# The LRU's eight input chunks in two sets of four beside the incoming shift and scale units

## The chip, the cores and the metric

One NeuronCore of one Trainium2 chip. The metric is the time of one execution on the device in microseconds; the median of three runs of the kernel before is 2256.2 us (2254.24 to 2256.78).

## The reference, cut to what matters

Two layers of a decoder trunk on 256 tokens of width 2048 in float32. Each layer has a token mixer and a squared-ReLU MLP, each with a layer norm behind it, and each is modulated by a shift, a scale and a gate that come from a condition vector. Layer 0's mixer is the recurrent block (RG-LRU), layer 1's a sparse attention. What the change touches is the first modulation and the recurrent block:

```python
mod = jnp.einsum('bd,jde->bje', cond, ada_w[layer]) + ada_b[layer]
shift, scale, gate = jnp.split(mod, 3, axis=-1)
h = x * (1.0 + scale[:, 0, None]) + shift[:, 0, None]
y_br, x_br = jnp.split(h @ w_in, 2, axis=-1)
xc = conv_b + sum(xp[:, k:k + seq] * conv_w[k] for k in range(CONV_WIDTH))
gates = jnp.einsum('bsnd,jnde->jbsne', xb, gate_w)
...
u = jnp.sqrt(-jnp.expm1(2.0 * log_a)) * (i * xc)
_, hs = lax.associative_scan(_linear_combine, (a, u), axis=1)
y = (jax.nn.gelu(y_br) * hs) @ w_out
x = _layer_norm(DN_ALPHA * x + (1.0 + gate[:, 0, None]) * y, ln_w[layer, 0], ln_b[layer, 0])
```

`xp` is x_br with three rows of zeros in front and `xb` is xc in eight blocks of 256 columns, each with its own gate matrices. The gates go through a sigmoid and become a and i.

## The kernel before

Every product is computed in float32 by three matmuls (`mm3`, L193): each operand is cut into a high part (rounded on ACT, L137 for weights, L529 for activations) and a low part (the difference, on VectorE, L138 and L530). A weight unit is 1 MB: four k tiles of 128 rows by 512 columns; a piece is one k tile of it. A unit lands in one of six raw slots (`RAW`), is cut in two halves of 1024 columns, and lies in a ring of 16 pieces (`RING`), four units, until TensorE has used it.

All DMAs are issued on SP's queue in the order of one list, `stream`. Its items are weight units ("w"), units of the modulation's weights ("a": one VectorE instruction, L120, multiplies a 1 MB unit with the condition and sums it, which gives 128 columns of a shift, scale or gate), units that TensorE multiplies directly ("p", L379, for the first gate), the recurrent gates' matrices ("n", L873), and loads that take no slot ("d": here x, L364). `Builder` walks a clock of its own (`step`, 1.31 us for a piece, 3 us for the arrival of a unit) to decide where in the program an item is consumed (`pump`) and when tasks go on (`spawn`, `until`). The compiler then orders each engine's queue by its own estimate; each engine works through its queue in that order.

For the LRU's input, the activation is h, transposed: 16 k tiles in groups (`GROUPS0`). For each group the stream has its shift units, its part of x, its scale units, and then the weight parts of four output chunks, two of x_br (4 and 5) and two of y_br (0 and 1). When a group's last scale unit is done, `modulate` (L478) makes scale and shift (L461 to L470), modulates x on ACT (L488) and splits it. `gemm_ws_outer` (L212) runs the four chunks group by group, all eight PSUM banks holding their sums. Then `conv_done` (L816) and `gelu_done` (L840) read the banks, and `gates` (L859) computes the recurrent gates of chunks 0 and 1: 16 matmuls into four banks, then Tanh, Exp and Sqrt on ACT and products and a scan on VectorE, ending in Q, the operand of lru_out. The other two chunk pairs follow, 16 k tiles each (L921 to L924), each with its gate block. Beside them stand the 16 units of the first gate and the 8 shift and scale units of the MLP's first group (`merge`, L345). lru_out (`proj`, L635) runs four column blocks of 512, with both row halves in turn per k tile, but in the last block one half after the other ("end"); 8 more shift and scale units stand beside it. The layer norm and the MLP follow.

Work tiles of 4 KB per partition come from one pool of 20 (`NS4`, L71); PSUM banks from two tags of four, "g" and "m".

## Time and profile before

| | |
|---|---|
| median of three runs | 2256.2 us |
| profiled execution, its own time | 2254.88 us |
| its span | 2253.1 us |
| TensorE busy | 2156.2 us, 96% |
| weight loads of TensorE busy | 1926.7 us, 86% |
| VectorE busy | 1638.1 us, 73% |
| ACT busy | 1059.4 us, 47% |
| moved by DMA | 625.02 MB, mean 277 GB/s |
| chain that ended last | TensorE 86%, VectorE 8%, ACT 2%, DMA 1% |

PE is TensorE, PEld its weight loads, DVE VectorE, SP the engine that issues the DMAs. Times are us from the first instruction. A busy share is an average over the whole span; what a wait costs is read where it stands. The duration that a row gives one instruction can reach a little into the next one's, so the distance from start to start is the shorter price. Tiles have the program's names without numbers: s is a work tile, g and m are PSUM banks, raw, whi and wlo a unit and its two parts.

### The profile page before, as it was taken

The numbers are of one execution on the slowest core, as the hardware profiler recorded it, in microseconds if no ns is written. First come the engines' busy times: TensorE is split into PE (matmuls) and PEld (weight loads), VectorE is DVE, ScalarE is ACT, GpSimd is POOL, SyncE is SP. The second block draws the span as 40 slices with busy tenths as digits, with TensorE's granted clock in tenths as the row PEclk, the third lists the DMA queues.
The fourth block names the chain that finished last, engine by engine and source line by source line (L and its number), as shares of the span: only waits on it lengthen the run. The fifth ranks groups of instructions, "written<-read, shape, count | busy, mean of one in ns | idle before, by whom it ended". The sixth has DMA issues, their size and how long they took to land.

```text
span 2253.1 us, 34112 instructions
## 1 busy us (share of the span) xinstructions
PE 2156.2 (96%) x14093; PEld 1926.7 (86%) x14093; DVE 1638.1 (73%) x1959; ACT 1059.4 (47%) x1387; POOL 0.2 (0%) x4
## 2 busy tenths in 40 slices
PE   3799999899999999999999999999999999999997
PEld 3788877898998898898779988788989988988986
DVE  8898788797777677778887688667777544554566
ACT  2356563554554454354453345536544544543541
POOL 0000000000000000000000000000000000000000
PEclk9899999999999999999999999999999999999999
DMA  9988878689888887889788866355888655555671
GB/s 396 414 325 340 346 298 334 262 351 383 332 308 300 304 330 288 298 303 338 256 300 348 332 249 248 122 206 184 285 330 303 215 197 187 192 198 190 213 255 38
DMA packets 98775, 625.02 MB, mean 277 GB/s; under 512 B 10963, under 2 KB 13443, under 8 KB 27452
## 3 DMA queue, kind: packets, MB, share of 16 engines
q1 hardware_dynamic: 98620, 622.85, 74.0%
q8 instruction: 110, 1.80, 0.3%
q14 instruction: 45, 0.37, 0.0%
HBM read 614.36 MB, written 8.45 MB: 276 GB/s over the span
## 4 chain that ended last, share of the span: by engine, by line
PE 86%; DVE 8%; ACT 2%; issue 2%; DMA 1%; SPq 0%; DVEq 0%; ACTq 0%
PE g L196 27%; PE g L197 27%; PE g L195 26%; DVE raw L120 4%; DVE wlo L138 2%; PE m L1167 1%; PE m L1133 1%; ACT whi L137 1%; DMA raw<-in_ada 1%; PE m L197 0%; PE m L195 0%; ACT s L488 0%; PE m L196 0%; PE g L873 0%; PE m L1159 0%
## 5 line engine op out<-in xcount | busy, mean ns | idle before, releaser
L138 DVE TENSOR_TENSOR wlo<-raw,whi 128x1024 fp32r<-128x1024 f32 x721 | 870.5, 1222 | 448.3 <-ACT whi L137 447.3
L137 ACT ACTIVATE whi<-raw 128x1024 fp32r<-128x1024 f32 x721 | 755.0, 1057 | 860.5 <-PE g L197 439.2
L195 PE MATMUL g<-s,whi 128*128 128x256 f32 (+1 forms) x2768 | 773.6, 280 | 58.6 <-ACT s L529 57.5
L196 PE MATMUL g<-s,whi 128*128 128x256 f32 (+1 forms) x2768 | 771.5, 279 | 3.2 <-DVE s L530 3.2
L197 PE MATMUL g<-s,wlo 128*128 128x256 f32 (+1 forms) x2768 | 770.1, 279 | 1.9 <-DVE wlo L138 1.8
L195 PEld LDWEIGHTS g<-s,whi 128*128 128x128 f32 (+1 forms) x2768 | 522.4, 189 | 73.0 <-ACT s L529 58.6
L195 PE MATMUL g<-whi,s 128*128 128x512 f32 x1376 | 541.4, 394 | 7.6 <-ACT s L529 4.2
L196 PE MATMUL g<-wlo,s 128*128 128x512 f32 x1376 | 543.1, 395 | 2.1 <-DVE wlo L138 2.1
L197 PE MATMUL g<-whi,s 128*128 128x512 f32 x1376 | 543.9, 396 | 0.3 <-DVE s L530 0.3
L196 PEld LDWEIGHTS g<-s,whi 128*128 128x128 f32 (+1 forms) x2768 | 522.8, 189 | 7.2 <-DVE s L530 4.7
L197 PEld LDWEIGHTS g<-s,wlo 128*128 128x128 f32 (+1 forms) x2768 | 522.6, 189 | 5.4 <-DVE wlo L138 4.2
L120 DVE SCALAR_TENSOR_TENSOR raw<-raw,one,cond 128x2048 f32<-128x2048 f32 x176 | 411.5, 2347 | 44.9 <-DMA raw<-in_ada 44.6
L195 PEld LDWEIGHTS g<-whi,s 128*128 128x128 f32 x1376 | 259.6, 189 | 67.8 <-ACT s L529 5.9
L196 PEld LDWEIGHTS g<-wlo,s 128*128 128x128 f32 x1376 | 259.9, 189 | 62.7 <-DVE wlo L138 2.5
L197 PEld LDWEIGHTS g<-whi,s 128*128 128x128 f32 x1376 | 260.0, 189 | 56.4 <-DVE s L530 1.8
L195 PE MATMUL m<-s,whi 128*128 128x256 f32 x256 | 70.5, 277 | 0.2 <-ACT whi L137 0.2
L197 PE MATMUL m<-s,wlo 128*128 128x256 f32 x256 | 70.6, 276 | 0.0
L196 PE MATMUL m<-s,whi 128*128 128x256 f32 x256 | 70.6, 276 | 0.0
L488 ACT ACTIVATE s<-s,hB,hA 128x256 f32<-128x256 f32 x32 | 16.7, 592 | 101.2 <-DVE hA L464 75.8
L530 DVE TENSOR_TENSOR s<-t,s 128x512 fp32r<-128x512 f32 x78 | 53.3, 686 | 4.0 <-ACT s L529 3.8
L708 ACT ACTIVATE t<-g 128x512 f32<-128x512 f32 x58 | 33.9, 587 | 33.0 <-PE g L197 33.0
L195 PEld LDWEIGHTS m<-s,whi 128*128 128x128 f32 x256 | 48.0, 188 | 0.4 <-ACT whi L137 0.4
(196 smaller groups left out, 1046.9 us busy)
## 6 DMA issues: line engine op xcount, KB each, us to landing
raw<-in_mlp_w SPq DMA_DIRECT2D x256, 1024.0 KB, 5.0
raw<-in_ada SPq DMA_DIRECT2D x176, 1024.0 KB, 6.8
raw<-in_lru_in SPq DMA_DIRECT2D x28, 1024.0 KB, 6.3
raw<-in_nsa_kv SPq DMA_DIRECT2D x24, 1024.0 KB, 5.0
raw<-in_gate SPq DMA_DIRECT2D x16, 1024.0 KB, 10.9
raw<-in_lru_out SPq DMA_DIRECT2D x16, 1024.0 KB, 6.6
raw<-in_nsa_q SPq DMA_DIRECT2D x16, 1024.0 KB, 6.2
raw<-in_nsa_out SPq DMA_DIRECT2D x16, 1024.0 KB, 5.2
```

Of the source, the lines that this page charges most:

```text
L120: nc.vector.scalar_tensor_tensor(r, r, self.one, self.cond, op0=OP.mult, op1=OP.mult, accum_out=it.col)
L137: nc.scalar.activation(hi, src, AF.Copy)
L138: nc.vector.tensor_tensor(out=lo, in0=src, in1=hi.bitcast(F32), op=OP.subtract)
L195: mm(out, lhi, rhi, start=start, stop=False, skip_group_check=True)
L196: mm(out, lhi, rlo, start=False, stop=False, skip_group_check=True)
L197: mm(out, llo, rhi, start=False, stop=stop, skip_group_check=True)
L488: SC.activation(x[:, j, :], x[:, j, :], AF.Identity, scale=hA[s][:, k:k + 1], bias=hB[s][:, k:k + 1])
L530: V.tensor_tensor(out=lo, in0=src, in1=hi.bitcast(F32), op=OP.subtract)
L708: SC.activation(r2, banks[b], AF.Relu)
L1133: T.matmul(ps, qT[:, h, 128 * t:128 * t + 128], kT[g // 2][:, g % 2, :, 0:K], start=True, stop=True)
L1167: T.matmul(po, vt[br][:, kt, 128 * g:128 * g + 128], pT[:, br, kt], start=first, stop=False)
```

## The change

The eight chunks make two sets (`SETS0`): chunks 4, 0, 5, 1 and chunks 6, 2, 7, 3. The first group of four k tiles becomes two of two, the last two of two become one of four. `PLAN0` gives the order on TensorE: set 0 over k tiles 0 to 3, set 1 over 0 to 3 and 4 to 7, set 0 over 4 to 15, set 1 over 8 to 15. A set that stops before its last k tile copies its banks into work tiles (ACT); when it ends, the rest is added to them (VectorE), and convolution and GELU then read the work tile, not PSUM. The stream has set 1's parts merged with the shift and scale units of the next groups. All four gate blocks follow the whole input, each with three of the first gate's units behind it and the last four at the end; a block waits in the builder's clock until the block two before it is finished (`fin`), and its square root goes into xc's tile. The MLP's first 8 shift and scale units move from beside the input to lru_out, which then has 16.

```diff
--- before.py
+++ after.py
@@ -33,7 +33,9 @@
 NS4 = 20
 NS2 = 6
 LNACT = (0, 2)
-GROUPS0 = ((0, 4), (4, 8), (8, 12), (12, 14), (14, 16))
+GROUPS0 = ((0, 2), (2, 4), (4, 8), (8, 12), (12, 16))
+SETS0 = ((4, 0, 5, 1), (6, 2, 7, 3))
+PLAN0 = ((0, GROUPS0[:2], False), (1, ((0, 4), (4, 8)), False), (0, GROUPS0[2:], True), (1, ((8, 12), (12, 16)), True))
 GROUPS1 = ((0, 4), (4, 8), (8, 12), (12, 16))
 UNIT_US = 3.0
 
@@ -225,6 +227,27 @@
                 if k1 == NK:
                     done(b)
 
+    def gemm_ws_sets(self, act, plan, kinds, part):
+
+        for q, groups, final in plan:
+            k_first, k_last = groups[0][0], groups[-1][1] - 1
+            bs = [None] * len(kinds)
+            for k0, k1 in groups:
+                for c, kind in enumerate(kinds):
+                    if k0 == k_first:
+                        bs[c] = [self.bank([128, 2, 256], kind) for _ in range(2)]
+                    b = bs[c]
+                    for k in range(k0, k1):
+                        ahi, alo = act(k)
+                        whi, wlo = self.piece(self.cons)
+                        for f in range(4):
+                            sl = slice(128 * f, 128 * f + 128)
+                            self.mm3(b[f // 2][:, f % 2, :], whi[:, sl], wlo[:, sl], ahi, alo, k == k_first and f % 2 == 0, k == k_last and f % 2 == 1)
+                        self.take()
+                        self.step(1.31)
+                    if k1 == k_last + 1:
+                        part(q, c, b, final)
+
     def gemm_as(self, act, done, stagger=None, kind="g"):
         b = [self.bank([128, 512], kind) for _ in range(2)]
         if not stagger:
@@ -400,24 +423,30 @@
     def w_part(name, ix, k0, k1):
         return Item("w", a[name][ix + (k0 // 4,)][:, 512 * (k0 % 4):512 * (k0 % 4) + 512 * (k1 - k0)], width=512 * (k1 - k0))
 
-    for k0, k1 in GROUPS0:
+    def w_set(q, k0, k1):
+        return [w_part("lru_in", (i,), k0, k1) for i in SETS0[q]]
+
+    def in_group(k0, k1):
         ks = range(k0, k1)
-        stream += ada_items(0, 0, ks)
-        if k0 % 4 == 0:
-            stream.append(x_item(k0 // 4))
-        stream += ada_items(0, 1, ks, hook(("h0", k0, k1)))
-        stream += [w_part("lru_in", (i,), k0, k1) for i in (4, 0, 5, 1)]
-    lru_in = [N("lru_gate", 0), N("lru_gate", 1)]
-    for c in (2, 3):
-        lru_in += [W("lru_in", 4 + c, g) for g in range(4)] + [W("lru_in", c, g) for g in range(4)] + [N("lru_gate", c)]
+        x = [] if k0 % 4 else [x_item(k0 // 4)]
+        return ada_items(0, 0, ks) + x + ada_items(0, 1, ks, hook(("h0", k0, k1)))
+
+    for k0, k1 in GROUPS0[:2]:
+        stream += in_group(k0, k1) + w_set(0, k0, k1)
+    stream += merge(w_set(1, 0, 4), in_group(4, 8))
+    stream += merge(w_set(1, 4, 8) + w_set(0, 4, 8), in_group(8, 12))
+    stream += merge(w_set(0, 8, 12), in_group(12, 16))
+    stream += w_set(0, 12, 16) + w_set(1, 8, 12) + w_set(1, 12, 16)
+    gate0 = gate0_items()
+    for c in range(4):
+        stream += [N("lru_gate", c)] + gate0[3 * c:3 * c + 3]
+    stream += gate0[12:]
     lru_out = [W("lru_out", n, g) for n in range(4) for g in range(4)]
     def ss_group(k0, k1):
         ks = range(k0, k1)
         return ada_items(1, 0, ks) + ada_items(1, 1, ks, hook(("h1", k0, k1)))
 
-    gate0, ss0 = gate0_items(), ss_group(*GROUPS1[0])
-    stream += merge(lru_in, [it for i in range(8) for it in (gate0[2 * i], ss0[i], gate0[2 * i + 1])])
-    stream += merge(lru_out, ss_group(*GROUPS1[1]))
+    stream += merge(lru_out, ss_group(*GROUPS1[0]) + ss_group(*GROUPS1[1]))
     for i, (k0, k1) in enumerate(GROUPS1):
         if i > 1:
             stream += ss_group(k0, k1)
@@ -858,7 +887,7 @@
 
     def gates(c):
         d = L[c]
-        B.until(lambda: "xs" in d)
+        B.until(lambda: "xs" in d and (c < 2 or "fin" in L[c - 2]))
         xc = d["xs"]
         banks = {}
         for b in range(2):
@@ -892,7 +921,7 @@
             SC.activation(e, e, AF.Copy, scale=0.5, bias=0.5)
             n = B.t4([128, 4, 256])
             V.scalar_tensor_tensor(n, tr, 1.0, e, op0=OP.add, op1=OP.mult)
-            sq = B.t4([128, 4, 256])
+            sq = xc
             SC.activation(sq, tr, AF.Sqrt)
             yield 1.3
             V.scalar_tensor_tensor(n, n, 2.0, e, op0=OP.subtract, op1=OP.mult)
@@ -913,14 +942,28 @@
             split(hi, lo, g2)
             for f in range(4):
                 Q[4 * c + f] = [hi[:, f, :], lo[:, f, :], 3]
+            d["fin"] = True
         B.spawn(task())
 
-    B.gemm_ws_outer(act, [conv_done(0), gelu_done(0), conv_done(1), gelu_done(1)], "ggmm", GROUPS0)
-    gates(0)
-    gates(1)
-    for c in (2, 3):
-        B.gemm_ws(act, conv_done(c))
-        B.gemm_ws(act, gelu_done(c))
+    sums = {}
+
+    def part(q, c, banks, final):
+
+        if not final:
+            sums[q, c] = B.t4([128, 4, 256])
+        t = sums[q, c]
+        halves = [t[:, 2 * b:2 * b + 2, :] for b in range(2)]
+        for o, p in zip(halves, banks):
+            if final:
+                V.tensor_tensor(out=o, in0=o, in1=p, op=OP.add)
+            else:
+                SC.activation(o, p, AF.Copy)
+        if final:
+            i = SETS0[q][c]
+            (conv_done(i - 4) if i >= 4 else gelu_done(i))(halves)
+
+    B.gemm_ws_sets(act, PLAN0, "ggmm", part)
+    for c in range(4):
         gates(c)
 
     z = [None] * 4
```

## Rows read from the trace of the kernel before

**Rows 1.** Windows: length, busy us (count) of PE, PEld, DVE, ACT, POOL; clock, DMA share, GB/s.
```profile
0.00:37.85 37.85, 0.00 (x1) 0.01 (x1) 29.20 (x71) 8.02 (x13) 0.20 (x4) 1.00 0.96 385
37.85:152.71 114.86, 97.29 (x768) 95.42 (x769) 105.20 (x120) 45.28 (x59) 0.00 (x0) 0.93 0.99 398
152.71:295.25 142.54, 136.21 (x1027) 114.87 (x1025) 111.64 (x136) 89.31 (x133) 0.00 (x0) 1.00 0.81 315
295.25:390.12 94.87, 92.79 (x384) 74.40 (x384) 84.97 (x92) 43.16 (x42) 0.00 (x0) 0.96 0.87 333
441.00:473.00 32.00, 32.00 (x283) 31.82 (x281) 25.42 (x30) 11.68 (x17) 0.00 (x0) 1.00 0.88 348
310.00:390.00 80.00, 80.00 (x344) 64.57 (x342) 70.19 (x77) 30.34 (x29) 0.00 (x0) 1.00 0.90 346
```

**Rows 2.** Waits of TensorE, 0 to 400 us: total, times, longest.
```profile
PE g L195 <- ACT s L529: 53.2, 4, 37.8
```

**Rows 3.** Chain that ended last, 20 to 48 us: start, us, what.
```profile
21.59 2.27 DVE raw L120 x2
...
24.31 9.09 DVE raw L120 x8
```

**Rows 4.** Timeline, 62 to 72.2 us: start, us, instruction, count, idle before and releaser.
```profile
65.68 0.08 DVE L120 DVE_READ_ACCUMULATOR raw<-raw,one,cond 128x1 f32 x1
...
66.20 2.07 ACT L488 ACTIVATE s<-s,hB,hA 128x256 f32<-128x256 f32 x4 [21.78 <-DVE hA L464]
68.18 1.04 ACT L137 ACTIVATE whi<-raw 128x1024 fp32r<-128x1024 f32 x1
...
69.25 1.23 DVE L138 TENSOR_TENSOR wlo<-raw,whi 128x1024 fp32r<-128x1024 f32 x1 [3.09 <-ACT whi L137]
...
70.22 0.79 PE L195 MATMUL g<-s,whi 128*128 128x256 f32 x2 [6.65 <-ACT s L529]
...
71.67 0.58 PE L196 MATMUL g<-s,whi 128*128 128x256 f32 x1 [0.66 <-DVE s L530]
```

**Rows 5.** Windows, clock after that wait; columns as in the first group.
```profile
68.40:75.20 6.80, 4.33 (x18) 4.03 (x19) 5.95 (x6) 6.80 (x8) 0.00 (x0) 0.50 1.00 400
```

**Rows 6.** Timeline of VectorE, 318 to 376 us.
```profile
318.85 4.63 DVE L138 TENSOR_TENSOR wlo<-raw,whi 128x1024 fp32r<-128x1024 f32 x4
...
367.06 1.39 DVE L665 TENSOR_TENSOR s<-g,s 128x512 f32<-128x512 f32 x2 [2.82 <-PE g L197]
368.37 1.28 DVE L670 SCALAR_TENSOR_TENSOR s<-t,s 128x512 f32<-128x512 f32 x2
...
370.76 4.62 DVE L138 TENSOR_TENSOR wlo<-raw,whi 128x1024 fp32r<-128x1024 f32 x4
```

**Rows 7.** Instructions of VectorE by line, 145 to 318 us: busy, mean ns | idle before.
```profile
L834 DVE SCALAR_TENSOR_TENSOR s<-g,cols,s 128x255 f32<-128x255 f32 (+2 forms) x36 | 14.3, 473 | 2.6 <-ACT s L832 2.6
L906 DVE TENSOR_TENSOR_SCAN s<-s,s 128x256 f32<-128x256 f32 x16 | 9.8, 672 | 0.0
L901 DVE TENSOR_TENSOR s<-s,s 128x1024 f32<-128x1024 f32 x4 | 4.9, 1224 | 0.3
```

**Rows 8.** Instructions of ACT by line, 145 to 318 us.
```profile
L886 ACT ACTIVATE s<-s,spm 128x256 f32<-128x256 f32 x16 | 9.0, 609 | 0.0
...
L883 ACT ACTIVATE s<-g,gb 128x256 f32<-128x256 f32 x16 | 6.8, 469 | 2.6 <-PE g L873 2.5
...
L846 ACT ACTIVATE s<-g 128x512 f32<-128x512 f32 x6 | 3.6, 596 | 30.5 <-PE g L197 30.3
```

**Rows 9.** Timeline of TensorE, fourth gate block and the gate unit behind it.
```profile
283.86 1.89 PE L873 MATMUL g<-s,raw 128*128 128x256 f32 x8
...
290.86 1.04 PE L379 MATMUL m<-raw,condT 128*1 128x512 f32 x8
```

**Rows 10.** Timeline of ACT in the same block: the table load and what follows.
```profile
299.00 1.28 ACT L896 ACT_TABLE_LOAD   x1
300.29 1.06 ACT L896 ACTIVATE s<-s 128x1024 f32<-128x1024 f32 x1
```

## The prediction

> **What bounds the kernel now.** I read the shares of busy time first, then the windows by stage, the waits of TensorE, and the chain and the timeline where TensorE stands still. TensorE is busy 96% of the span, so all there is to win is its idle time and the stretches at the lower clock. The windows [rows 1] say where these are. Before 37.85 us TensorE does nothing. In the first stage (to 152.71, the first four input chunks beside the 32 shift and scale units) it is busy 97.3 of 114.9 us, VectorE 105.2, and the DMA engines are at 0.99. In the second (gates, chunks 2 and 3, to 295.25) it is busy 136.2 of 142.5, in the third (lru_out, to 390.12) 92.8 of 94.9: there TensorE is the bound.
>
> TensorE's waits in the first stage end with the rounded activation: 53.2 us in four waits, 37.8 of it at the start [rows 2]. The chain shows what stands before that: eight shift and scale products per four k tiles on VectorE, 2.27 us each (9.09 for four) [rows 3]. The timeline has the end of a group: ACT modulates for 2.07 us, rounds a weight, rounds the activation; VectorE waits 3.09 us meanwhile, and TensorE comes 6.65 us after its last matmul [rows 4], with a granted clock of 0.50, the lower level of 1.2 GHz, for the next 6.8 us [rows 5]: 3.4 us lost. A group on VectorE is 8 x 2.27, four weight units at 2.3 (four halves take 4.63 [rows 6]), and 4.6 for the wait, the sums and the activation's low part: 32.0 us. From 37.8 to 70.2 the trace has 32.4, so this sum is some 0.4 short per group. The first stage is a queue on VectorE, with the DMA close behind.
>
> **The change, part by part.** Times count from the start of the profiled span (2253.1 us; that execution's own time is 2254.9, the median of the runs 2256.2, so 1.3 is added at the end).
>
> (1) First groups of two k tiles. Four shift and scale units instead of eight stand before the first matmul; the fourth ends at 23.9 [rows 3], and with half the modulation TensorE starts near 27, not 37.85. Worth 0 by itself: it only comes earlier to the next wait for the same queue.
>
> (2) VectorE up to the last of the 32 units. Behind the fourth stand 28 units (63.6 us), 20 weight units (45.8; 8 more than before stand ahead of this point), and the ends of two short groups (3.1 each) and two long ones (4.6): 23.9 + 63.6 + 45.8 + 15.4 + 4 x 0.4 = 150.5. The DMAs to there, in order on SP's one queue, are 54 units of 1.05 MB and 1.5 MB of constants; 385 GB/s to 37.85 and 398 after it [rows 1] bring them by 147: hidden, by 3 us. TensorE's part is five groups of 192 matmuls at 0.113 (283 in 32 us [rows 1]), 21.7 us each, between 27 and 151: hidden.
>
> (3) The rest of the input. The first matmul of set 0's last group comes 4.5 us behind the last unit (65.76 to 70.22 [rows 4]), at 155, and streams 1.45 later; three groups are left, 65.1, and 3.4 go to the lower clock after the wait. The input ends at X = 225. In these 70 us VectorE has 12 weight units, 12 adds, and nearly all the convolutions and GELUs (48 x 0.39 [rows 7] and 16 x 0.61), some 57 us: here it is idle, and nothing in the stream can use that.
>
> (4) The parked sums. 16 copies out of PSUM on ACT, 0.60 each by the square of that size [rows 8]: 9.5 us, hidden as ACT is busy 45.3 of 114.9 [rows 1]; a copy that still waits for TensorE holds what is behind it on ACT, the next weight's rounding (rival C). The next set's first matmul needs the banks of a copy issued two or more chunks earlier: 0. 16 adds on VectorE at 0.61 to 0.70 (L665, out of PSUM, has this shape [rows 6]): 10.5 us, most of it in the idle time of (3); 2 are taken on the path, in (5). The convolutions and GELUs now read SBUF: 0, bounds -3 and +3, since L665 out of PSUM and L670 out of SBUF stand as close [rows 6]. The reuse of xc takes a tile away, `fin` orders the emission: 0; without the spare tiles a gate block would wait for the one two before it, some 20 us on its chain.
>
> (5) Four gate blocks and 16 gate units in one piece. TensorE: 4 x 7.0 and 16 x 1.0 [rows 9], 44 us. DMA: 20 units through six slots, six of them landed by X; the first slot comes free at X + 7, and 14 more units and lru_out's first weight take 15 x 2.63 (1.05 MB at 398 GB/s): landed at X + 46.4, split by X + 47.7. So the DMA ends this stage, 4 us behind TensorE. ACT per block: Tanh and Exp (9.0 each for L886 and its twin L887, 6.8 for L883 and as much on its other banks, over four blocks [rows 8]) 7.9, four whole-tile passes 4.2, two table loads 2.6: 14.7, some 13 as the instructions overlap. VectorE: 7 x 1.14 + 4 x 0.6 = 10.4 [rows 7]. Four blocks are 52 us of ACT, the last Q is ready near X + 60, and the unit of lru_out that needs it is split at X + 64: hidden by 4 us.
>
> A rule of the Trainium skill speaks against four blocks in a row. First the row: a table load takes 1.28 us, and the next activation starts 0.01 behind its end [rows 10]. The page "ScalarE: Activation LUTs" (section What ACT_TABLE_LOAD costs) counts a drain of 1380 ns more for a switch; by it the eight switches would take 11 us more and the last Q would come at X + 71. This trace has no such drain.
>
> (6) lru_out with 16 shift and scale units beside it instead of 8 (the other 8 leave the second stage, and on SP's queue one now stands between every two weights). TensorE: 384 x 0.233 (344 in 80 us [rows 1]), 89.5. DMA: 30 units and 2.5 MB of x and gate rows behind the first weight, last one at X + 132. VectorE from X + 47.7 to the last weight half: 16 x 2.3, 15 x 2.27, 18 x 0.61 (gate product, residual, statistics of three column blocks), 9.3 left of the last gate block and 2.4 of gate row: 93.4. So VectorE sets this stage: the last weight is split at X + 141, the first row half ends 1.3 later, and the second takes 48 x 0.233 = 11.2. lru_out ends at X + 153.6 = 378.6. Before, it ended at 390.1, with the last weight split at 375.4 [rows 6] and TensorE the bound. The last unit now stands among the layer norm's instructions: 2 us.
>
> Sum: 378.6 + 2 - 390.1 = -9.5. Behind that the work is the same. 2254.9 - 9.5 + 1.3 = 2247 us. A check on it: VectorE was busy 331.0 of these 390.1 us [rows 1]; with the adds it would be 341.5 of 380.6. Its idle 59 us fall to 39, of which the change can spend no more without filling the gap in (3).
>
> **The rivals.**
>
> A: VectorE's waits at the groups' ends go, because a landed weight of the other set stands behind them. Four waits of 2 to 3.1 us, and part of the 3.4: X = 213, 12 us less, 2235. For: the merged stream has such a weight at each group's end. Against: before, a weight stood there too, and ACT had been idle for 21.8 us [rows 4], yet it was rounded only behind the modulation.
>
> B: no net change. With the blocks in one piece VectorE waits for ACT, and if the last Q comes 9 us later than X + 60, the 93 us of (6) stretch by as much: lru_out ends near 388, 2256 (2252 to 2260). For: ACT's 13 us per block against TensorE's 10 to 11, with the rounding for lru_out on top. Against: 41 us of VectorE in 47 leave the chains room.
>
> C: slower, by ACT's order. In set 1's second group the units come every 4.6 us (a weight and a shift and scale unit). If a chunk's copy stands ahead of the next weight's rounding, that rounding waits for 5.4 us of matmuls, for the first half's rounding and low part ahead of them and for the copy: 7.7 per chunk, 3.1 more, 12.5 for four, and some 4 at set 0's short groups, where TensorE is at the lower clock. VectorE's queue is the bound there, so all of it comes through: 2247 + 16 = 2263. It is slower than before once the eight copies cost over 1.2 us each (the 9.5), and so by more than 0.2% from 1.8. For: ACT works in order, and its squares before did wait 30.5 us for TensorE [rows 8]. Against: the unit between two weights gives the next rounding time to stand first.
>
> **How the numbers follow.** About 0.2%, 4.5 us, is what a measurement here can tell from no change. The forecast (2240 to 2251) has 0.40, A (2228 to 2239) 0.20, B 0.22, C 0.18. Faster: forecast and A, 0.60; within: B, 0.22; slower: C, 0.18. The time is the forecast's 2247; the range goes over most of A and of C: 2232 to 2262.
>
> **What would show it.** (1) First matmul near 27 us. (2) The last L120 of these 32 units ends near 151; near 163, with ACT waiting at the copies, it is C; near 140, A. (3) The first L873 near 225, and VectorE idle some 13 us before it. (5) The first lru_out matmul near 273, behind the weight's DMA. (6) TensorE waits for the weights' low parts in the last column block, and the last lru_out matmul is near 379. If lru_out runs without waits and ends near 365, VectorE was not its bound; if it ends past 388, the gate blocks cost more than I gave them.

## The result: slower, and the profile after

2269.5 us, median of four executions (2266.7 to 2274.2), against 2255.2 (2252.7 to 2256.8): ratio 1.0067, 95% interval 1.0045 to 1.0088. Two further measurements gave 1.0063 (1.0044 to 1.0082) and 1.0059 (1.0047 to 1.0071). The forecast was 2247, the range ended at 2262. The profiled execution took 2267.6 us, its span is 2265.8.

Windows by stage of the changed kernel, columns as in [rows 1]: ahead of the first matmul; to set 0's last group; to the input's end; gate blocks; lru_out; layer norm; the MLP's first outer stage. The last row is a stretch inside the third and fourth.

```profile
0.00:28.38 28.38, 0.00 (x1) 0.01 (x1) 21.04 (x64) 7.65 (x12) 0.20 (x4) 1.00 0.92 347
28.38:163.84 135.46, 118.56 (x960) 116.43 (x961) 115.33 (x116) 57.35 (x74) 0.00 (x0) 0.96 0.98 394
163.84:233.00 69.16, 68.51 (x580) 68.13 (x581) 63.06 (x100) 38.06 (x48) 0.00 (x0) 0.96 0.61 223
233.00:299.00 66.00, 49.35 (x267) 30.00 (x266) 51.69 (x56) 59.19 (x95) 0.00 (x0) 0.84 0.80 323
299.00:392.40 93.40, 87.47 (x371) 70.35 (x371) 82.59 (x88) 28.46 (x29) 0.00 (x0) 0.98 0.90 362
392.40:415.70 23.30, 7.76 (x34) 6.55 (x32) 17.57 (x39) 16.33 (x25) 0.00 (x0) 0.62 0.58 235
415.70:512.90 97.20, 92.69 (x768) 91.89 (x769) 84.39 (x84) 44.16 (x54) 0.00 (x0) 0.95 0.86 329
213.00:239.00 26.00, 26.00 (x204) 25.20 (x203) 19.95 (x41) 11.81 (x22) 0.00 (x0) 1.00 0.20 71
```

Before, the last two stages were:

```profile
390.12:405.43 15.31, 5.63 (x32) 5.15 (x33) 8.13 (x27) 11.88 (x21) 0.00 (x0) 0.78 0.46 161
405.43:497.16 91.73, 89.41 (x768) 88.82 (x769) 82.84 (x82) 45.10 (x56) 0.00 (x0) 0.98 0.86 338
```

Length less TensorE's busy time is its idle time. Before [rows 1]: 37.9 + 17.6 + 6.3 + 2.1 + 9.7 + 2.3 = 75.8 us. After: 28.4 + 16.9 + 0.7 + 16.7 + 5.9 + 15.5 + 4.5 = 88.6. The 9.5 us of the early start are there; 10.3 go again up to lru_out, 3.8 in lru_out, 5.9 in the layer norm, 2.2 behind it. That is 12.7 more, and the spans differ by 12.7. That the two agree to the tenth is chance: busy time up to the outer stage's end is 424.3 against 421.3, and 3.0 come back later. TensorE was busy at the lower clock for 42.1 us up to there, against 23.1 before; part of what that costs was given back by a faster pace of the matmuls, of which below.

Waits of TensorE after, 0 to 600 us (columns as in [rows 2]):

```profile
PE g L197 <- ACT s L558: 45.3, 8, 28.4
PE m L611 <- ACT s L596: 13.9, 2, 7.2
PE g L198 <- DVE wlo L140: 10.0, 5, 4.0
PE g L197 <- ACT whi L139: 8.2, 1, 8.2
...
PE m L402 <- DMA raw<-in_gate: 4.3, 3, 1.5
```

The first answers to [rows 2]: 28.4 instead of 37.8 at the start. The wait for the DMA is new and the other three are larger than before (6.4, 2.1 and 4.4 us), and each has its place.

**The input.** Timeline of ACT, 90 to 113 us, and under it VectorE's:

```profile
92.40 1.28 ACT L960 ACTIVATE s<-g 128x512 f32<-128x512 f32 x2 [6.29 <-PE g L199]
93.57 3.90 ACT L139 ACTIVATE whi<-raw 128x1024 fp32r<-128x1024 f32 x4
97.84 1.28 ACT L960 ACTIVATE s<-g 128x512 f32<-128x512 f32 x2 [0.37 <-PE g L199]
103.28 1.28 ACT L960 ACTIVATE s<-m 128x512 f32<-128x512 f32 x2 [4.16 <-PE m L199]
104.45 2.00 ACT L139 ACTIVATE whi<-raw 128x1024 fp32r<-128x1024 f32 x2
108.72 1.28 ACT L960 ACTIVATE s<-m 128x512 f32<-128x512 f32 x2 [2.27 <-PE m L199]
109.89 3.90 ACT L139 ACTIVATE whi<-raw 128x1024 fp32r<-128x1024 f32 x4
```
```profile
105.54 2.36 DVE L140 TENSOR_TENSOR wlo<-raw,whi 128x1024 fp32r<-128x1024 f32 x2 [1.30 <-ACT whi L139]
110.98 2.36 DVE L140 TENSOR_TENSOR wlo<-raw,whi 128x1024 fp32r<-128x1024 f32 x2 [3.08 <-ACT whi L139]
```

ACT waits for TensorE's last matmul of a chunk, copies (L960), and only then rounds the next weight; VectorE waits behind it. This is the place that rival C named. Then the DMA stands: from 213 to 239 us it is at 0.20, with all six slots full of gate units and gate weights that no engine can use yet.

**The gate blocks.** ACT at the last block's end:

```profile
284.21 1.28 ACT L925 ACT_TABLE_LOAD   x1
285.50 1.06 ACT L925 ACTIVATE s<-s 128x1024 f32<-128x1024 f32 x1
286.99 1.06 ACT L929 ACTIVATE s<-s 128x1024 f32<-128x1024 f32 x1 [0.43 <-DVE s L927]
287.95 1.99 ACT L139 ACTIVATE whi<-raw 128x1024 fp32r<-128x1024 f32 x2
```

lru_out's first weight is rounded behind the whole fourth block, 55 us after the input's end at 233; ACT was busy 59.2 of the 66 us from 233 to 299.

**The layer norm.** VectorE, the second row half's product with the gate (L694), its residual (L699) and its normalization (L602):

```profile
392.87 0.68 DVE L694 TENSOR_TENSOR s<-g,s 128x512 f32<-128x512 f32 x1
...
393.54 1.20 DVE L140 TENSOR_TENSOR wlo<-raw,whi 128x1024 fp32r<-128x1024 f32 x1
...
399.44 2.34 DVE L122 SCALAR_TENSOR_TENSOR raw<-raw,one,cond 128x2048 f32<-128x2048 f32 x1
...
404.20 0.69 DVE L699 SCALAR_TENSOR_TENSOR s<-t,s 128x512 f32<-128x512 f32 x1
...
409.38 1.00 DVE L602 TENSOR_SCALAR s<-s,mv,r 128x512 f32<-128x512 f32 x2
```

Before, the same three:

```profile
390.44 0.63 DVE L665 TENSOR_TENSOR s<-g,s 128x512 f32<-128x512 f32 x1
...
391.11 0.68 DVE L670 SCALAR_TENSOR_TENSOR s<-t,s 128x512 f32<-128x512 f32 x1
...
397.92 1.00 DVE L573 TENSOR_SCALAR s<-s,mv,r 128x512 f32<-128x512 f32 x2
```

The residual followed its product after 0.67 us; now 11.3 lie between, with six weight halves, the first row half's normalization and the last shift and scale unit.

### The profile page after: what moved, and what is told of

It reads as the page before. It is cut to its first block, busy times and chain, and to the rows that moved or that the text cites. A ratio compares the mean times of both kernels' runs of the same rounds, so it can differ in the third digit from the quotient of the medians.

```text
span 2265.8 us, 34162 instructions
## 1 busy us (share of the span) xinstructions
PE 2156.0 (95%) x14093; PEld 1928.6 (85%) x14093; DVE 1650.5 (73%) x1975; ACT 1069.7 (47%) x1403; POOL 0.2 (0%) x4
## 3 DMA queue, kind: packets, MB, share of 16 engines
q1 hardware_dynamic: 98620, 622.85, 73.5%
## 4 chain that ended last, share of the span: by engine, by line
PE 83%; DVE 9%; ACT 4%; DMA 2%; issue 1%; SPq 0%; DVEq 0%; ACTq 0%
PE g L198 25%; PE g L199 25%; PE g L197 25%; DVE raw L122 3%; DVE wlo L140 2%; DMA raw<-in_ada 1%; PE m L197 1%; PE m L198 1%; PE m L199 1%; PE m L1210 1%; PE m L1176 1%; ACT whi L139 1%; ACT s L517 1%; ACT s L912 0%; DMA t<-in_lnrow 0%
## 5 line engine op out<-in xcount | busy, mean ns | idle before, releaser
L197 PE MATMUL g<-s,whi 128*128 128x256 f32 x2640 | 738.6, 281 | 45.3 <-ACT s L558 45.3
L198 PE MATMUL g<-s,whi 128*128 128x256 f32 x2640 | 737.4, 279 | 4.6 <-DVE s L559 4.6
L199 PE MATMUL g<-s,wlo 128*128 128x256 f32 x2640 | 736.1, 279 | 0.7 <-DVE wlo L140 0.7
L197 PEld LDWEIGHTS g<-s,whi 128*128 128x128 f32 x2640 | 499.7, 190 | 51.4 <-ACT s L558 46.9
L198 PEld LDWEIGHTS g<-s,whi 128*128 128x128 f32 x2640 | 500.6, 190 | 8.5 <-DVE s L559 5.9
L199 PEld LDWEIGHTS g<-s,wlo 128*128 128x128 f32 x2640 | 500.8, 190 | 1.2 <-DVE wlo L140 0.9
L199 PE MATMUL m<-s,wlo 128*128 128x256 f32 x384 | 105.4, 276 | 1.3 <-DVE wlo L140 1.3
L197 PE MATMUL m<-s,whi 128*128 128x256 f32 x384 | 106.2, 278 | 0.2 <-ACT whi L139 0.2
L198 PE MATMUL m<-s,whi 128*128 128x256 f32 x384 | 105.8, 276 | 0.0
L199 PEld LDWEIGHTS m<-s,wlo 128*128 128x128 f32 x384 | 71.8, 188 | 1.5 <-DVE wlo L140 1.5
L197 PEld LDWEIGHTS m<-s,whi 128*128 128x128 f32 x384 | 72.4, 189 | 0.4 <-ACT whi L139 0.4
L198 PEld LDWEIGHTS m<-s,whi 128*128 128x128 f32 x384 | 72.1, 188 | 0.0
```

The costliest lines, as they stand in the source:

```text
L197: mm(out, lhi, rhi, start=start, stop=False, skip_group_check=True)
L198: mm(out, lhi, rlo, start=False, stop=False, skip_group_check=True)
L199: mm(out, llo, rhi, start=False, stop=stop, skip_group_check=True)
```

## The experiments

Marks of all profiles, in us: the start of the input's last matmul, lru_out's length from its 25th matmul (the first behind 24) to its last, the time from its last matmul to the MLP's first (layer norm), that matmul, TensorE's idle time up to there. Each is of one execution; between the changed kernel's three profiles (after, e6, e18) they differ by up to 2.5 us. Then the median of all executions, and the ratio to the kernel before measured with it, with the 95% interval; this ratio weighs the single executions and is not the quotient of the medians.

| run | input | lru_out | norm | MLP | idle | us | ratio |
|---|---|---|---|---|---|---|---|
| before | 283.7 | 83.8 | 15.7 | 405.4 | 73.5 | 2255.2 | |
| after | 232.2 | 90.8 | 23.3 | 415.7 | 84.1 | 2269.5 | 1.0067 (1.0045-1.0088) |
| e1 | 224.7 | 90.9 | 23.3 | 408.3 | 75.3 | 2271.6 | 1.0055 (1.0033-1.0078) |
| e2 | 240.0 | 84.1 | 13.3 | 416.4 | 82.9 | 2269.1 | 1.0040 (1.0019-1.0061) |
| e3 | 283.0 | 93.1 | 21.4 | 416.9 | 83.0 | 2270.6 | 1.0062 (1.0035-1.0088) |
| e4 | 280.4 | 83.8 | 23.3 | 401.2 | 71.8 | 2257.4 | 0.9998 (0.9977-1.0019) |
| e5 | 232.7 | 91.4 | 23.3 | 416.8 | 81.9 | 2270.8 | one execution |
| e6 | 230.5 | 91.0 | 23.3 | 414.0 | 84.5 | 2269.7 | 1.0063 (1.0044-1.0082) |
| e7 | 231.6 | 100.6 | 13.6 | 415.8 | 82.1 | 2273.1 | one execution |
| e8 | 244.8 | 89.9 | 23.3 | 412.5 | 77.5 | 2269.7 | 1.0056 (1.0041-1.0071) |
| e9 | 291.2 | 86.6 | 14.5 | 408.0 | 74.3 | 2259.4 | 1.0020 (1.0009-1.0031) |
| e10 | 233.5 | 91.4 | 23.3 | 418.0 | 85.9 | 2270.0 | 1.0059 (1.0039-1.0078) |
| e11 | 249.0 | 91.1 | 23.3 | 418.4 | 84.6 | 2268.0 | 1.0056 (1.0036-1.0077) |
| e12 | 232.4 | 90.5 | 22.2 | 414.9 | 80.1 | 2261.9 | one execution |
| e13 | 259.3 | 82.2 | 19.3 | 420.5 | 84.7 | 2271.6 | 1.0074 (1.0057-1.0091) |
| e14 | 230.3 | 90.9 | 19.4 | 409.4 | 79.3 | 2272.8 | 1.0065 (1.0044-1.0087) |
| e15 | 249.6 | 88.9 | 20.3 | 414.4 | 76.8 | 2271.4 | 1.0069 (1.0047-1.0091) |
| e16 | 280.7 | 83.7 | 21.1 | 399.1 | 73.1 | 2250.9 | 0.9974 (0.9953-0.9995) |
| e17 | 243.2 | 90.3 | 19.4 | 408.1 | 72.8 | 2267.8 | 1.0046 (1.0030-1.0061) |
| e18 | 230.7 | 91.0 | 23.3 | 414.2 | 82.1 | 2268.1 | 1.0059 (1.0047-1.0071) |

**e1: no copies.**

```diff
-                SC.activation(o, p, AF.Copy)
+                G.memset(o, 0.0)
```

> The changed kernel with the 16 copies of the partial sums out of PSUM left out (the parked tiles are set to zero on GpSimd instead, so the partial sums of the first pass are lost). Theory (the copies hold weight roundings behind them on ACT, about 9 us of VectorE's wait up to the last of the 32 shift and scale units): that unit ends near 150.5 instead of 159.4, the input ends 8 to 9 us earlier (near 224 instead of 233), and the time falls by 7 to 10 us, to about 2261. Rival (the DMA, at 0.98 of the stretch, would hold the same unit anyway): the unit ends no earlier than 156 and the time falls by less than 3 us, 2266 to 2270.

VectorE's wait for rounded weights up to 160 us, first in the changed kernel, then without copies, with the last of the 32 units:

```profile
DVE wlo L140 <- ACT whi L139: 17.5, 9, 3.1
```
```profile
DVE wlo L140 <- ACT whi L139: 12.5, 6, 3.1
149.75 2.35 DVE L122 SCALAR_TENSOR_TENSOR raw<-raw,one,cond 128x2048 f32<-128x2048 f32 x1
```

The unit ends 7.3 us earlier than in the changed kernel (152.0 against 159.3), the input and the MLP's first matmul 7.5 and 7.4; against e6 and e18, where the unit ends at 158.2, it is 6 us each time. The copies cost that: the theory for the marks. The time did not fall (2271.6), as the rival had it; of that below.

**e5: copies later.**

```diff
-                SC.activation(o, p, AF.Copy)
+        if not final:
+            def task():
+                yield 6.0
+                for o, p in zip(halves, banks):
+                    SC.activation(o, p, AF.Copy)
+            B.spawn(task())
```

> The changed kernel with the 16 copies of the partial sums issued 6 us later in the kernel's own clock, so that more weight roundings stand ahead of them on ACT (nothing is left out). Theory (a copy that waits for TensorE holds the roundings behind it): part of what the kernel without copies gained comes back, the input ends at 226 to 230 instead of 232.5 and the MLP's first matmul comes 3 to 6 us earlier, 410 to 413. Rival (the copies cost by their number, not by their place): the input ends at 231 to 234 and nothing moves.

Input 232.7, MLP 416.8: nothing moved, the rival's numbers. The delay put several chunks' copies in a row. ACT's waits at copies up to 160 us fell from 17.4 to 8.8 us, but its waits for weights to land rose from 23.8 to 33.3, and two copies still stood ahead of a rounding (4.2 and 2.3 us). So e1 shows what the copies cost; that it is their place on ACT and not their number is read from the timeline and not shown by an edit.

**e9, e10: the early start alone, and the change without it.**

```diff
-GROUPS0 = ((0, 4), (4, 8), (8, 12), (12, 14), (14, 16))
+GROUPS0 = ((0, 2), (2, 4), (4, 8), (8, 12), (12, 16))
```

> The kernel before with one part of the change alone: its first two groups have two k tiles instead of four (and the last one four). Theory (the early start is worth nothing, as TensorE then waits for the same queue on VectorE, and what the sets and the gate blocks cost is elsewhere): the first matmul near 28 us, TensorE stands still 9 us less ahead of it and as much more in the first stage, the MLP's first matmul within 4 us of 405.4, the time within 4 us of the kernel before. Rival (all versions with the sets begin their matmuls at 28 us, and a TensorE that begins in short pieces loses more to its lower clock and its slower pace later): 8 us or more slower than before, 2264 and up.

> The changed kernel with the early start undone: the first group is four k tiles again (one group of set 0 before set 1's two), all else as changed. Theory (the early start is worth nothing): the first matmul at 37.8 us, the MLP's first matmul and the time within 4 us of the changed kernel, 2266 to 2274. Rival (the early start itself costs): 8 us or more faster than the changed kernel, 2262 or less.

Alone it costs 3.9 us (1.0020): behind the first wait for the activation TensorE waits four times, 31.7 us, instead of three times, 15.4 [rows 2]. Undone in the changed kernel it is worth nothing. Step (1), "worth 0 by itself", holds there; alone it is slightly worse, just inside the 4 us that were expected.

**e3, e8, e11: gate blocks two and two.** e3 moves all 16 gate units between the sets as well; e8 and e11 move the blocks' own weights alone (the lines of the stream are left out here). e8 has e5's copies too, e11 the first group of before.

```diff
-    B.gemm_ws_sets(act, PLAN0, "ggmm", part)
-    for c in range(4):
-        gates(c)
+    B.gemm_ws_sets(act, PLAN0[:3], "ggmm", part)
+    gates(0); gates(1)
+    B.gemm_ws_sets(act, PLAN0[3:], "ggmm", part)
+    gates(2); gates(3)
```

> The changed kernel with gate blocks 0 and 1 and all 16 gate units between the two sets (set 0 ends, two gate blocks, set 1 ends, two gate blocks) instead of all four blocks at the end. Theory (four blocks in a row are bound by ACT, 13.4 us a block, and the first rounding of lru_out stands behind the last block): two blocks of ACT lie beside 43 us of input matmuls, so lru_out streams some 15 to 20 us earlier (276 to 284 instead of 299), and the time falls by what VectorE's queue in lru_out lets through, 8 to 16 us: 2253 to 2262. Rival (lru_out is bound by VectorE's 93 us whatever stands before it, and the stretch of the gates is bound by the gate units' DMA): under 4 us.

> The changed kernel with the copies 6 us later and gate blocks 0 and 1 between the two sets (their two weights alone; all 16 gate units stay beside blocks 2 and 3). Theory (four blocks in a row are bound by ACT's 13.4 us a block, and lru_out's first rounding stands behind the last of them): only 27 us of ACT stand behind the input's end, lru_out streams from 278 to 284 instead of 299, the MLP's first matmul comes at 398 to 405, and the time is within 4 us of the kernel before or lower, 2250 to 2260. Rival (VectorE's work from 164 us to lru_out's end sets that end in any order): lru_out starts earlier and ends at 388 or later, and the time stays at 2264 or more.

> The changed kernel with two edits together: the first group of four k tiles, as before, and gate blocks 0 and 1 between the two sets (copies where the change has them). Theory (the input's ends of groups and the four blocks in a row are what costs): TensorE stands still 8 us less up to lru_out's end than in the changed kernel, that end near 386, the time 5 to 9 us below the changed kernel. Rival (what TensorE's idle time gives back comes back as lower clock and slower pace, as it did with the blocks two and two): the time stays at 2266 to 2274.

lru_out's 25th matmul: 301.6 in the changed kernel, 302.5, 299.3 and 304.0 here, and no time fell: the theory missed in all three. With ACT relieved, the gate units' DMA takes its place; TensorE waits for them for 7.9 us in e8. Windows of e8:

```profile
250.00:280.00 30.00, 23.88 (x145) 10.94 (x144) 16.50 (x17) 24.21 (x41) 0.00 (x0) 0.89 0.91 374
280.00:290.00 10.00, 5.88 (x26) 0.81 (x26) 8.56 (x11) 4.12 (x4) 0.00 (x0) 0.60 1.02 423
```

Both bounds of step (5) stand close together: less of the one leaves the other.

**e2, e13: eight shift and scale units early.** e2 puts them beside the last twelve input weights, e13 beside the last eight, and in e8. Of e2's edit:

```diff
-    stream += w_set(0, 12, 16) + w_set(1, 8, 12) + w_set(1, 12, 16)
+    stream += merge(w_set(0, 12, 16) + w_set(1, 8, 12) + w_set(1, 12, 16), ss_group(*GROUPS1[0]))
-    stream += merge(lru_out, ss_group(*GROUPS1[0]) + ss_group(*GROUPS1[1]))
+    stream += merge(lru_out, ss_group(*GROUPS1[1]))
```

> The changed kernel with the first eight shift and scale units of the first MLP read beside the last twelve input weights (where the DMA stood still from 213 to 239) instead of beside lru_out. Theory (lru_out's end is set by VectorE's queue and the units among the layer norm): lru_out's VectorE queue gets 18 us shorter, TensorE is the bound there, lru_out ends near 389 instead of 392.8, the first matmul of the MLP comes 8 to 12 us earlier (404 to 408), and with the lower clock shorter the time falls by 10 to 16 us, to 2254 to 2260. Rival (the start of lru_out behind the gate blocks sets everything, and the rest is TensorE): under 4 us, 2266 to 2270.

> The kernel with the copies 6 us later and the gate blocks two and two, and with it the first eight shift and scale units beside set 1's last eight weights instead of beside lru_out. Theory (VectorE's work is what is left, and in the stretch where lru_out waits for the gate units' DMA it is idle): lru_out runs at TensorE's pace (84 to 86 us from its 24th matmul), the layer norm takes 13 to 17 us instead of 23, the MLP's first matmul comes at 400 to 407 and the time is within 5 us of the kernel before, 2251 to 2261. Rival (VectorE was full at 83 of 86 us where the units now go): the input and the gate blocks end later by the 18 us that lru_out saves, and the time stays at 2265 or more.

In e2 lru_out runs with 0.5 us of waits and the layer norm takes 13.3 us, but the input ends 7.8 us later, and the MLP's first matmul stays. Where the units went, VectorE has no room (window of e2):

```profile
163.84:240.25 76.41, 71.67 (x577) 70.60 (x578) 76.41 (x109) 37.60 (x49) 0.00 (x0) 0.92 0.80 297
```

The prediction had 13 us of idle VectorE in this stretch; the window after shows 6.1 (69.16 less 63.06). e13 went the rival's way: lru_out takes 82.2 us, but its input ends at 259.3 (244.8 in e8) and the MLP starts at 420.5.

**e4: the eight units moved, alone.** In the kernel before:

```diff
-    stream += merge(lru_in, [it for i in range(8) for it in (gate0[2 * i], ss0[i], gate0[2 * i + 1])])
-    stream += merge(lru_out, ss_group(*GROUPS1[1]))
+    stream += merge(lru_in, gate0_items())
+    stream += merge(lru_out, ss_group(*GROUPS1[0]) + ss_group(*GROUPS1[1]))
```

> The kernel before with one part of the change alone: the eight shift and scale units that stood beside the gates and chunks 2 and 3 are read beside lru_out (16 there instead of 8). Theory (the units at lru_out's end stand among the layer norm's instructions on VectorE and delay the second half's transposes by 8 us, and the lower clock that follows costs some 5 more): slower than before by 8 to 14 us, 2263 to 2269. Rival (as predicted, 2 us in the layer norm, and lru_out's queue on VectorE of 93 us just as long as TensorE's): 0 to 4 us slower, 2255 to 2259.

The layer norm takes 23.3 us instead of 15.7, the theory's mechanism and its size, but lru_out begins and ends 11.8 us earlier (its last matmul at 377.9 against 389.7), and the MLP's first matmul comes 4.2 us earlier. The time is that of before (0.9998; the interval would hide these 4 us), so the theory's 8 to 14 us did not come. With 16 units beside it lru_out still takes 83.8: VectorE's amount of work is not what stretches it to 91.

**e7, e12, e14: what stretches lru_out and the layer norm.** e7 puts the 16 units beside the first 12 weights (`merge(lru_out[:12], ...) + lru_out[12:]`), e12 halves the products, e14 changes the planner's clock.

```diff
 # e12, for the 16 units beside lru_out (cut = 1024)
-nc.vector.scalar_tensor_tensor(r, r, self.one, self.cond, ...)
+nc.vector.scalar_tensor_tensor(r[:, :it.cut], r[:, :it.cut], self.one, self.cond[:, :it.cut], ...)
 # e14, for gate units, lru_out and the 16 units (us = 2.4)
-self.arrive.append(max(last, self.now + 1.5) + UNIT_US * it.width / 2048)
+self.arrive.append(max(last, self.now + 1.5) + it.us * it.width / 2048)
```

> The changed kernel with the 16 shift and scale units beside lru_out spread over its first 12 weights instead of all 16, so that none stands at its end. Theory (the last unit and the weight roundings stand ahead of the second row half's residual on VectorE and delay the layer norm): from lru_out's end to the MLP's first matmul 15 to 17 us instead of 22.9, and that matmul at 408 to 411. Rival (VectorE's queue of lru_out is as long in any order): lru_out ends later by what the layer norm saves, and the MLP's first matmul stays within 2 us of 415.7.

> The changed kernel with the 16 shift and scale products beside lru_out over 1024 of their 2048 columns (so these shifts and scales are sums over half the columns): VectorE has 16 x 1.1 = 18 us less to do there, the DMA and the order of the queues are the same. Theory (VectorE's queue stretches lru_out and the layer norm): from lru_out's 24th matmul to its last 84 to 87 us instead of 91, and from there to the MLP's first matmul 15 to 20 us instead of 23; that matmul at 405 to 411 instead of 414 to 416. Rival (the DMA behind its stand of 26 us at the input's end sets the pace of lru_out): 90 us or more for lru_out, and the MLP's first matmul within 2 us of the changed kernel.

> The changed kernel with 2.4 us instead of 3.0 in the kernel's own clock for the transfer of a gate unit, a lru_out weight and the 16 shift and scale units beside it: the same instructions on the same data, in another order on VectorE and ACT. Theory (the order of VectorE's queue stretches lru_out and the layer norm): from lru_out's last matmul to the MLP's first 14 to 17 us instead of 23.3, lru_out itself 84 to 90 us instead of 91, the MLP's first matmul at 402 to 408 and the time 6 to 13 us below the changed kernel, 2256 to 2264. Rival (the stand of the DMA and the gate blocks set the end in any order): the MLP's first matmul within 3 us of 415.7 and the time at 2266 or more.

e7: norm 13.6, lru_out 100.6, MLP 415.8; the rival. e12: with 18 us less to do on VectorE, lru_out takes 90.5 and the MLP's first matmul comes at 414.9; the theory falls, and the numbers are those of the rival, the DMA. Waits of VectorE in lru_out, in the changed kernel and with half the products:

```profile
DVE s L694 <- PE g L199: 10.5, 3, 4.4
```
```profile
DVE s L698 <- PE g L200: 23.3, 3, 9.9
```

The work taken away became waiting: the gate product of a column block waits in VectorE's queue for the block's last matmul, with the next weights' low parts behind it, and then TensorE waits for those (10.0 us in five waits above, 9.0 here). So the trace points at the order, in lru_out as in the layer norm, but no edit shows it for lru_out. The DMA is not excluded either: ACT rounds lru_out's weights as they land and waits for that for 46.5 us in the changed kernel, 51.3 in e12, 27.5 in e4; the DMA's queue in turn waits for slots that VectorE frees (66.3 and 64.5 us from 299 to 392.4 in the first two). e14 has the residual 0.67 us behind its product again; its norm takes 19.4 us, not 14 to 17, since weight halves still lie between, and its lru_out is 90.9, no shorter than before the edit. The MLP's first matmul comes at 409.4, 4.6 to 6.3 us earlier than in the changed kernel's profiles and later than the theory's 402 to 408: the rival's "in any order" falls for the layer norm, its time holds.

**e15, e16: the same clock in e8 and in e4.** The edit is e14's; in e16 it is for lru_out and its 16 units only.

> The version with the copies 6 us later and the gate blocks two and two, and in it 2.4 us instead of 3.0 in the kernel's own clock for the gate units, lru_out's weights and the 16 units beside it. Theory (the gains add up: 3 to 5 us of TensorE's idle time before lru_out's end, 8 in the layer norm): the MLP's first matmul at 400 to 405, 2252 to 2260. Rival: as for the run with the order alone, 2264 or more.

> The kernel before with the eight units moved beside lru_out, and in it 2.4 us instead of 3.0 in the kernel's own clock for lru_out's weights and the 16 units beside it. Theory (the order of VectorE's queue is what stretched the layer norm to 23.3 us there): the layer norm takes 14 to 17 us, the MLP's first matmul comes at 392 to 396, and the time is 5 to 9 us below the kernel before, 2246 to 2251. Rival (the unit work itself): 23 us and 2255 to 2259, as without it.

e15 missed: MLP 414.4, 2271.4 us. e16's median is 2250.9 us beside 2253.7 of the kernel before, ratio 0.9974, the interval just below 1: clearly faster than the changed kernel, and hardly shown to be faster than the kernel before. The theory missed in the marks: the norm takes 21.1 us instead of 14 to 17, the MLP comes at 399.1 instead of 392 to 396, 2.1 us earlier than in e4, so what e16 gained is not shown to be the order. Windows of its lru_out and layer norm:

```profile
288.80:378.40 89.60, 88.73 (x388) 72.02 (x384) 85.21 (x98) 40.79 (x44) 0.00 (x0) 1.00 0.92 354
378.40:399.10 20.70, 5.22 (x33) 4.84 (x32) 13.52 (x32) 11.74 (x21) 0.00 (x0) 0.75 0.61 230
```

**e6, e18: the changed kernel again; e17: e1, two and two, and e14's clock together.**

> The changed kernel once more, beside the kernel before on the same chip, as a control. Theory (its loss is in the stages up to the MLP's first outer stage): the same marks within 2 us, the input's end at 232.5 and the MLP's first matmul at 415.7, and 2264 to 2275 us. Rival (the difference between the two kernels came from TensorE's pace in single executions, 113 or 118 ns per matmul): the marks move by more than 4 us and the time falls within 4 us of the kernel before.

> The changed kernel without the copies (the first pass's partial sums are lost), with the gate blocks two and two and with 2.4 us for a unit in the kernel's own clock. Theory (the gains add up and the time follows TensorE's idle time): the input and lru_out end 8 to 12 us earlier than in the changed kernel, the MLP's first matmul comes at 396 to 404, and the median time is 10 to 15 us below the changed kernel beside it, 2255 to 2260. Rival (what TensorE's idle time gives back is lost again in slower stretches later): the same marks, but the median within 5 us of the changed kernel's.

> The changed kernel a third time, as the control beside it. Both theories: the MLP's first matmul at 414 to 416 and a median of 2267 to 2272 us; its executions lie up to 8 us apart with the marks up to there within 2 us, by the matmuls' pace of 113 or 118 ns.

The controls agree in marks and time. e17 cut TensorE's idle time up to the MLP from 82.1 to 72.8 us, below that of the kernel before, and its median is 2267.8 beside 2268.1. Its marks came later than either theory had them (MLP 408.1 instead of 396 to 404), but for the time the rival holds: in these versions it did not follow TensorE's idle time. Where it went in the profiled execution, two rows each of the first measurement and of e18, and one of e17, show:

```profile
600.00:688.00 88.00, 87.98 (x770) 87.49 (x769) 65.11 (x61) 45.48 (x54) 0.00 (x0) 1.00 0.80 301
776.00:868.00 92.00, 92.00 (x792) 91.09 (x791) 66.58 (x61) 48.07 (x57) 0.00 (x0) 1.00 0.79 296
```
```profile
600.00:688.00 88.00, 88.00 (x746) 87.82 (x745) 65.40 (x61) 43.16 (x53) 0.00 (x0) 1.00 0.79 299
776.00:868.00 92.00, 92.00 (x791) 91.11 (x790) 66.61 (x63) 48.26 (x58) 0.00 (x0) 1.00 0.78 295
```
```profile
776.00:868.00 92.00, 92.00 (x772) 91.53 (x772) 63.31 (x58) 45.64 (x55) 0.00 (x0) 1.00 0.79 298
```

From 600 to 688 it is the same kernel in the same stretch, busy throughout at the same granted clock, and 3% fewer matmuls: most 256-column matmuls start 113.3 ns apart in the one execution and 117.8 in the other (512-column ones 228.9 and 233.3). Every distance from start to start at the full clock, counted above the faster pace, adds up to 21 us in e17's profile, 15 in e1's, 4 in the changed kernel's first, 10 in e6's, 8 in e18's and 9 in that of the kernel before. So e1 and e17 lost in their profiled executions what they had gained in idle time. e17's was the slowest of its six; whether the other executions had as much of this pace no trace shows, and what sets it was not found. It stays open.

The lower clock is the other part. Over all executions the mean granted clock is 0.985 to 0.990 for the kernel before and 0.979 to 0.987 for every version with the sets. In the profiles TensorE was busy at 1.2 GHz for 30.3 us before, for 46.8, 34.3 and 43.5 in the changed kernel's three, and for 50.7 in e17. About half of that is lost (an estimate: a 512-column matmul took 0.43 us at that clock, from 299 to 303 us before, and 0.229 at the full one), so 14 us before and 16 to 22 in the changed kernel.

## Why the prediction was wrong

The early start and the landing of lru_out's first weight were right. What failed are the costs that were put at nothing or too low: the copies in (4), a rounding that stands behind the gate blocks in (5), and the weight halves and the unit ahead of the residual in (6). Measured end to end it missed by 22.2 us of span (12.7 more instead of 9.5 less), and the marks add up to it: lru_out's end 14.2 late, the layer norm 5.6, the outer stage 5.4, less 3.0 behind it.

- Step (1) right: the first matmul at 28.4 against "near 27", worth nothing (e10).
- Step (2) failed, by a term that was left out: "150.5" has no copies in it (its terms add up to 150.3). Measured 159.3; without copies 152.0. Rival C named the copies; they cost 6 to 7.5 us at the input's end, not its 16. X came to 233 instead of 225.
- Step (3): VectorE's idle time was 6.1 us, not 13, so e2 had nowhere to put work. The terms named there, taken in full, come to 64 us and not to "some 57"; 63.1 were measured.
- Step (4) failed: it put the copies down as hidden, since ACT was busy 45.3 of 114.9 us. ACT's share says nothing of what stands behind a copy that waits.
- Step (5) failed at "split by X + 47.7". The weight was issued at 270.6 and landed near X + 47 (an estimate, by the median of 9.4 us from issue to landing there), as forecast, but its rounding started at X + 55, behind the fourth block on ACT, and its first low part was ready at X + 61. Rival B named the engine, and half of what it needed came: the last Q was ready at 298.5, X + 65.5, so 5.5 us behind X + 60 and not 9. The drain that "ScalarE: Activation LUTs" (What ACT_TABLE_LOAD costs) in the Trainium skill counts would have given X + 71; the load at 284.21 is followed after 0.01 us, so the delay was the queue and not a drain.
- Step (6): 93.4 us from the first split weight to the last was nearly met (92.4, from 294.3 to 386.7), by luck: the amount of VectorE's work did not set it (e12, e4). What did, the order of its queue or weights that landed late, stays open. The rate of 0.233 us per matmul [rows 1] was itself one of a slow stretch: 96 matmuls of the changed kernel's lru_out without a wait take 22.0 us, 0.229 each.
- "The last unit now stands among the layer norm's instructions: 2 us" failed: 7.6, as not the unit alone but six weight halves stand ahead of the residual.
- Nothing was put down for the outer stage, and 3.4 us in all for the lower clock. The stage took 97.2 us instead of 91.7 here, at a mean granted clock of 0.95, but 92.9 and 92.5 in the two later profiles, where the clock was 0.98: the stretch at 0.50 behind the layer norm lasted to 421.8 here and to 412.7 and 413.0 there.

The early start's 9.5 us was real, and so was e4's earlier lru_out. The first was paid for in TensorE's next waits for the same queue, 7.6 of e4's 11.8 us in the layer norm.

Why the time itself is 0.6% above that of before is shown only in part: the marks say where TensorE stood still, but no edit of the changed kernel that moved them brought the median back.

## What to carry to other kernels

Before a move is costed at nothing because an engine has idle time, write down what stands behind the moved instruction in that engine's queue and who waits for that: here an engine that waited at one instruction started nothing behind it (ACT 6.3 us ahead of a copy, VectorE 4.4 us ahead of a gate product). Where a program plans its order by a clock of its own, a unit time there can matter more than the amount of work: 2.4 instead of 3.0 us shortened the layer norm by 3.9 us (e14), 18 us less work by 1.1 (e12). And when idle time is taken away and the median stays, compare counts of matmuls in equal busy windows before looking for another wait.

## What was not expected of the hardware

TensorE ran with two paces at the same granted clock of 1.00, 113.3 and 117.8 ns from start to start of 256-column matmuls, for stretches of 40 to 180 us; in e18 one stretch began at 595 us, where a stage changes, and ended at 775. By the distances from start to start it cost 4, 10 and 8 us in three profiles of the changed kernel and 21 in e17's, as much as what was to be explained. For an isolated matmul the Trainium skill, "TensorE: Matmul & The Clock Gate" (Back-to-back issue gap), gives N / 2.4 + 2.5 ns, by which an estimate for these is 109.2, and it says that in a stream of weight loads and matmuls both set the spacing. The profiles have one weight load for each matmul (14093 of both), and both measured paces are slower than that estimate.
